# The values of a gated linear attention as one unit of seven half products

## The chip, the core and the metric

The kernel runs on one core of a Trainium2 chip, in one launch. The metric is the device time in microseconds (us). Times of the kernel before are the median of three runs; durations and waits are read from one further execution that the hardware profiler recorded.

## The reference: what is computed

One layer of an encoder over 1024 tokens of 1024 features: a normalisation, one projection into queries, keys, values and gates, a gated linear attention of four heads in both directions, a pooling branch, a merge, and a feed-forward layer. The part that matters here:

```
h = rmsnorm(x, norm_mix)                       # 1024 tokens x 1024 features
q, k, v, r, lr_f, lr_b, u, g_a, g_b = split(h @ w_in)
#   q, k: 4 heads x 128;  v: 4 heads x 256 = 1024 columns
log_a_f = log_sigmoid(lr_f @ w_decay_up_fwd + b_decay_fwd) / 16      # and _b
o_fwd = gla_chunked(q, k, v, log_a_f)          # scan over chunks of tokens
o_bwd = flip(gla_chunked(flip(q), flip(k), flip(v), flip(log_a_b)))
# in each chunk:  o = (q_e k_e^T, masked) v + q_e S ;  S <- decay * S + k_d^T v
o = rmsnorm of o_fwd + o_bwd, times gla_norm * silu(r);   y_a = o @ w_branch_gla
```

All inputs and the output are float32. The values `v = h @ w_v` are a product of 1024 x 1024 by 1024 x 1024: this is the product that the change rebuilds.

## The kernel before

**Exact products from pairs.** TensorE multiplies in a shortened float type (`F32R`). Each operand is therefore kept as a high part and a low part: `split_to` (lines 200 to 202) has ScalarE (ACT) cast the tile to the high part (line 201), and then VectorE (DVE) or GpSimd (POOL) subtracts it to give the low part (line 202; for weights it is POOL, for most activations DVE). A product of two tiles is then three matmuls onto one PSUM bank, high x high, high x low, low x high: `products` and `mm3` (lines 270 to 277; line 273 is the matmul). In names `wh` and `wl` are high and low parts of weights, `hh` and `hl` of the normalised features, `trh` and `trl` of sums of features, `vh` and `vl` of values. The low part is wanted by the second or third matmul of each three.

**Order of the work.** Every engine runs its instructions in the order of the program. SyncE (SP) issues the DMA transfers, also in order, each with its waits. TensorE's order is written out by hand: loops over heads and token tiles. After each three matmuls `mm3` calls `pump` (line 162 on), which counts the time by units of one such product of 512 columns (about 0.7 us) and lets side work be issued: `pending` (splits of weights, one each 2 units), `aside` (a list of sums with casts and stores beside them), `side` (generators that yield the number of units to their next step, such as `attention`), and `put_off` (`soon`: one step after a delay). So a `yield 6.5` in `attention` places the next step 6.5 products later in every engine's queue.

**Storage.** Tiles of 128 x 1024 come from 39 rotating slots (`slots`). Weights stand in `wts` with 6 buffers for each of high and low and 4 raw ones. PSUM has 3 banks for products (`ps_mm`) and 5 for the rest (`ps_g`).

**The stages around the change.** The features `hT` are made first, feature-major (high and low), two token tiles at a time. Values of heads 0 and 1 (`pair_products`, lines 494 to 502) are computed as plain products, token tiles 0 to 3 while the features are still being made: 8 row blocks x 3 matmuls into one bank of 128 tokens x 512 columns, and `keep_values` (480 to 492) splits the bank into high (ACT, line 490) and low (DVE, line 492) for both heads. Then `first_qk` (1181 to 1197) makes the low-rank decay inputs (`low_rank`, 541 to 553) and queries and keys of head 0: four banks of 8 x 3 matmuls. Beside its second half runs `sums_behind`: `feature_sums` (683 to 706) lets VectorE add high and low parts of the features and form sums and differences of the blocks (128 x 1024 each, recorded with line 768, names `hs`), which are stored to HBM (`f_out`) for the gates' seven-product units much later. After that `attention(0)` begins as side work, token tiles 7, 6 and 5 to 4 of the values of heads 0 and 1 follow on TensorE, and `store_block` stores one block of the features. Then `sum_pieces` (beside the heads 1 and 2) makes sums of weights of the later stages on POOL (names `wsum` and `rraw`, line 768). `project_qk` (line 895 on) makes queries and keys of heads 1 to 3. The values of heads 2 and 3 come after head 2's queries and keys, from `ValueWeights` (line 793 on): eight tiles of 24 matmuls.

`attention(h)` (from line 926) runs through: decays (matmuls `z`, line 935, then absolute value, exponential and logarithm on ACT, with the `yield 6.5` behind), scans on DVE (`decay`, from 958), exponentials (`exponentials`, 981 to 990), the factors applied to keys and queries (`apply_decay`, 992 to 999: keys on DVE, `qe` and `fac` on POOL) spaced by `HOLD` units, the transposed keys (`kt`, split at line 202), the backward states (`advance`, from 1020, which needs the values of its chunk), the scores with `SCORES` units behind them, and the outputs. Before a chunk whose value tile is not there yet it yields until it is.

## Time and profile before

| | us |
|---|---|
| runs | 1361.23, 1361.35, 1362.74 |
| median | 1361.35 |
| profiled execution, its own time | 1361.08 |
| its span in the trace | 1359.4 |
| TensorE busy | 1348.2 |
| DVE busy | 850.1 |
| POOL busy | 813.4 |
| ACT busy | 652.0 |

The span goes from the first to the last instruction that the profiler recorded; the execution's own time is 1.7 us longer. The granted TensorE clock was 0.999 of full speed. An instruction is listed with its start, its length, its engine, the line, the operation, the output and input tiles, and in square brackets the time that the engine waited before it and for whom. A group row has the count, the busy time and the mean length in ns, then the idle time ahead of its instructions and what ended most of it. Matmul lengths in the list overlap: two that follow each other start closer than one is long.

### The profile page before, as it was taken

To read this page: it belongs to the slowest core of one execution; us is meant where nothing else is said; L and a number is where in the kernel's file an instruction comes from. 1 tells how busy PE (TensorE), PEld (TensorE's weight loads), DVE (VectorE), ACT (ScalarE), POOL (GpSimd) and SP (SyncE) were. 2 spreads that over 40 slices of the span, in tenths; PEclk is the share of its full clock that TensorE was granted. 3 is DMA by queue.
4 is the path that set the end of the run, shared out by engine and by line. 5 is a ranking of instruction groups with operands and counts; after the bars stand their busy time and mean duration, and the time that the engine had idled before them with its cause. 6 is when DMAs were issued, how large, how long until landed. Compare 5 with 4: busy or idle time off the path is not lost. (4 is left out here: it accounts for less than half of the span.)

```text
span 1359.4 us, 18038 instructions
## 1 busy us (share of the span) xinstructions
PE 1348.2 (99%) x6226; PEld 1121.4 (82%) x6226; DVE 850.1 (63%) x1049; ACT 652.0 (48%) x1184; POOL 813.4 (60%) x626
## 2 busy tenths in 40 slices
PE   9999999999999999999999999999999999999998
PEld 7888888888888888888887888888888888888886
DVE  6975667766436868669774955565565655343375
ACT  7365666776435445453356533333333333444253
POOL 3333847586686548568853476666667666555463
PEclk9999999999999999999999999999999999999999
DMA  7243647446896669986327454555554447975552
GB/s 229 106 146 113 187 138 219 143 143 205 265 303 218 206 212 333 384 333 243 101 78 260 131 165 147 164 178 178 178 177 141 133 143 261 394 283 186 173 215 78
DMA packets 194621, 268.26 MB, mean 197 GB/s; under 512 B 13112, under 2 KB 121184, under 8 KB 194528
## 3 DMA queue, kind: packets, MB, share of 16 engines
q1 hardware_dynamic: 194384, 266.83, 58.6%
q8 instruction: 49, 0.80, 0.2%
q14 instruction: 44, 0.36, 0.1%
q10 hardware_dynamic: 144, 0.26, 0.1%
HBM read 178.70 MB, written 88.34 MB: 196 GB/s over the span
## 5 line engine op out<-in xcount | busy, mean ns | idle before, releaser
L202 POOL TENSOR_TENSOR wl<-fs,wh 128x512 fp32r<-128x512 f32 x120 | 165.9, 1386 | 155.8 <-ACT wh L201 99.7
L273 PE MATMUL ps<-gh,wh 128*128 128x512 f32 x616 | 240.5, 390 | 0.0
L273 PE MATMUL ps<-gl,wh 128*128 128x512 f32 x616 | 239.8, 389 | 0.3 <-DVE gl L1870 0.3
L273 PE MATMUL ps<-gh,wl 128*128 128x512 f32 x616 | 239.7, 389 | 0.0
L202 POOL TENSOR_TENSOR wl<-fraw,wh 128x512 fp32r<-128x512 f32 x90 | 129.5, 1439 | 57.4 <-ACT wh L201 52.2
L202 POOL TENSOR_TENSOR ol<-gor,oh 128x1024 fp32r<-128x1024 f32 (+1 forms) x42 | 101.6, 2423 | 85.7 <-ACT oh L201 59.7
L273 PEld LDWEIGHTS ps<-gl,wh 128*128 128x128 f32 x616 | 115.7, 188 | 24.4 <-DVE gl L1870 0.7
L273 PEld LDWEIGHTS ps<-gh,wl 128*128 128x128 f32 x616 | 115.6, 188 | 24.1
L273 PEld LDWEIGHTS ps<-gh,wh 128*128 128x128 f32 x616 | 115.7, 188 | 24.0 <-DVE sums L2036 0.2
L273 PE MATMUL ps<-hh,wh 128*128 128x512 f32 x296 | 119.8, 405 | 0.4 <-ACT ga L1654 0.4
L202 POOL TENSOR_TENSOR wl<-wraw,wh 128x512 fp32r<-128x512 f32 x56 | 93.3, 1693 | 44.8 <-ACT wh L201 44.7
L273 PE MATMUL ps<-oh,oh 128*128 128x512 f32 x308 | 119.8, 389 | 0.0
L273 PE MATMUL ps<-ol,oh 128*128 128x512 f32 x308 | 119.8, 389 | 0.0
L273 PE MATMUL ps<-oh,ol 128*128 128x512 f32 x308 | 119.8, 389 | 0.0
L273 PE MATMUL ps<-hh,wl 128*128 128x512 f32 x296 | 115.5, 390 | 0.0
L273 PE MATMUL ps<-hl,wh 128*128 128x512 f32 x296 | 115.5, 390 | 0.0
L202 DVE TENSOR_TENSOR ol<-wor,oh 128x1024 fp32r<-128x1024 f32 (+1 forms) x42 | 62.7, 1504 | 67.7 <-ACT oh L201 55.2
L273 PE MATMUL ps<-trh,wh 128*128 128x512 f32 x224 | 88.9, 397 | 0.0
L273 PE MATMUL ps<-trh,wl 128*128 128x512 f32 x224 | 87.2, 389 | 0.0
L273 PE MATMUL ps<-trl,wh 128*128 128x512 f32 x224 | 87.2, 389 | 0.0
L201 ACT CAST wh<-fs 128x512 fp32r<-128x512 f32 x120 | 73.7, 614 | 26.7 <-DVE fs L1239 25.8
L201 ACT CAST oh<-wor 128x1024 fp32r<-128x1024 f32 (+1 forms) x42 | 41.1, 978 | 63.6 <-PE ps L273 24.2
(286 smaller groups left out, 3153.3 us busy)
## 6 DMA issues: line engine op xcount, KB each, us to landing
fraw<-in_w_ffn_in_dram SPq DMA_DIRECT2D x44, 512.0 KB, 6.9
gor<-g_out SPq DMA_DIRECT2D x35, 512.0 KB, 4.6
g_out<-s SPq DMA_DIRECT2D x44, 256.0 KB, 2.4
fraw<-in_w_in_dram SPq DMA_DIRECT2D x20, 512.0 KB, 5.7
wor<-t_out SPq DMA_DIRECT2D x20, 512.0 KB, 4.5
g_out<-g SPq DMA_DIRECT2D x33, 256.0 KB, 2.9
x<-in_x_dram SPq DMA_DIRECT2D x16, 512.0 KB, 4.5
wor<-in_w_ffn_out_dram SPq DMA_DIRECT2D x15, 512.0 KB, 7.7
```

Of the source, the lines that this page charges most:

```text
L201: nc.scalar.copy(hi, src)
L202: eng.tensor_tensor(lo, src, as_f32(hi), op=ALU.subtract)
L273: nc.tensor.matmul(ps, a[i], b[j], start=first and n == 0, stop=last and n == 2, skip_group_check=onto)
```

## The change

The values of all heads become one unit of Strassen's scheme (Winograd's form): the token tiles are two halves, the features two halves, and the 1024 columns two halves (heads 0 and 1, heads 2 and 3). Seven half products, each 4 token tiles x 4 row blocks x 512 columns, with sums of feature blocks and sums of weight blocks as operands, replace eight.

- Products 1 and 2 together are the plain values of token tiles 0 to 3 for heads 0 and 1, made at the start as before. Product 1's sum is now also copied out of the bank half way (`keep_first`, ScalarE), since other products need it.
- `values((5, 3, 6))` follows head 0's queries and keys, `values((7, 4))` head 1's. 5, 6 and 7 start new banks, 3 and 4 go on in the banks of the product before. `v_evict` adds a finished bank to the kept rows on VectorE or ScalarE, with a few sums on POOL.
- The weight sums of products 5, 7, 6 and 3 are made by `value_sums` on POOL: 16 sums of 128 x 512 (line 865 in the changed kernel), beside the second half of head 0's queries and keys. Of products 5 and 3 they stay on the chip, of 6 and 7 they are stored and reloaded.
- The feature sums are the same that the gates use. VectorE's list of them is reordered so that number 5 comes first; they are stored, reloaded (`load_sums`), cast on ACT (`cast_sum`) and their low parts made on POOL (`low_sum`, `trl`, line 768 of the changed kernel).
- Values of heads 1 to 3 are stored to HBM (`v_raw`), reloaded by `load_values` in their head's attention, cast on ACT (`high_values`) and their low part made on POOL (`low_values`, line 1059 of the changed kernel).
- The sums of weight pieces (`rraw`, `wsum`) begin at product 7, the `rraw` pieces first, instead of behind token tile 4.
- The block of features stored by `store_block` is stored at product 3 and reloaded in heads 1 and 2.
- In `attention`, `HOLD` goes from 5 to 4, `SCORES` from 6 to 5.5, the wait behind the logarithms from 6.5 to 4 units.
- `ValueWeights` and its stage of 8 tiles x 24 matmuls after head 2 are gone.

In counts of instructions: TensorE has 48 matmuls fewer (6106 to 6058), POOL 50 two-input operations more (579 to 629), ACT 16 copies and 2 casts more, VectorE 8 two-input operations fewer (732 to 724), SP 53 transfers more (758 to 811).

How the queues change is shown at three places. The first is POOL from the low parts of head 0's key weights (`wl_674` and `wl_684` before, `wl_684` and `wl_694` after) on. Before:

```order
L202 TENSOR_TENSOR wl_674<-raw_629,wh_673 128x512
L202 TENSOR_TENSOR wl_684<-raw_631,wh_683 128x512
L202 TENSOR_TENSOR wl_771<-raw_753,wh_770 128x512
L202 TENSOR_TENSOR wl_781<-raw_755,wh_780 128x512
L998 TENSOR_TENSOR qe_948<-qe_948,q_588 128x512
L999 TENSOR_TENSOR fac_949<-fac_949 128x4
```

After; `vsum` and `vraw` are the weight sums, `wl_806` and `wl_816` the low parts of head 1's query weights, `trl_787` and `trl_788` the low parts of the feature sums of product 5, and `wl_842` the low part of its first weight block:

```order
L203 TENSOR_TENSOR wl_694<-raw_641,wh_693 128x512
L865 TENSOR_TENSOR vsum_703<-vsum_699,vsum_703 128x512 x2
L865 TENSOR_TENSOR vsum_705<-vsum_701,vsum_705 128x512 x2
L865 TENSOR_TENSOR vsum_699<-vraw_140,vsum_699 128x512 x2
L865 TENSOR_TENSOR vsum_701<-vraw_143,vsum_701 128x512 x2
L865 TENSOR_TENSOR vraw_140<-vsum_703,vraw_140 128x512
L203 TENSOR_TENSOR wl_806<-raw_783,wh_805 128x512
L203 TENSOR_TENSOR wl_816<-raw_785,wh_815 128x512
...
L768 TENSOR_TENSOR trl_787<-trl_787,trh_835 128x1024
L768 TENSOR_TENSOR trl_788<-trl_788,trh_838 128x1024
L203 TENSOR_TENSOR wl_842<-vsum_703,wh_841 128x512
L203 TENSOR_TENSOR wl_846<-vsum_703,wh_845 128x512
```

Twelve sums and two large low parts have come in between; the rows left out are three of the sums. On TensorE the same place, the end of head 0's keys (`ps_798` before, `ps_849` after) and what follows. Before, the plain values of token tile 7:

```order
L273 MATMUL ps_798<-hh_600,wl_684 128x512
L273 MATMUL ps_833<-wv_214,hh_494 128x512 x2
L273 MATMUL ps_833<-wv_214,hl_495 128x512
L935 MATMUL z_838<-lrT_538,up_158 128x512
L273 MATMUL ps_833<-wv_227,hh_494 128x512 x2
```

After, product 5, with its four banks side by side and `z` the decays of head 0:

```order
L274 MATMUL ps_849<-hh_597,wl_694 128x512
L274 MATMUL ps_892<-wh_841,trh_835 128x512
L274 MATMUL ps_892<-wl_842,trh_835 128x512
L274 MATMUL ps_892<-wh_841,trl_787 128x512
L1071 MATMUL z_904<-lrT_543,up_158 128x512
L274 MATMUL ps_891<-wh_841,trh_835 128x512
```

The weights `wv` that stood on the chip since the start are replaced by `wh_841` and `wl_842`, made on the spot, and the second matmul of product 5 reads `wl_842`. The third place is POOL in attention of head 1. Before, where `wsum` are the pieces of the later stages and `wl` the value weights of heads 2 and 3 or the next head's:

```order
L998 TENSOR_TENSOR qe_1642<-qe_1642,q_1042 128x512
L999 TENSOR_TENSOR fac_1643<-fac_1643 128x4
L768 TENSOR_TENSOR wsum_1379<-wsum_1379 128x256
L768 TENSOR_TENSOR wsum_1600<-wsum_1600 128x256
L998 TENSOR_TENSOR qe_1685<-qe_1685,q_1042 128x512
L999 TENSOR_TENSOR fac_1686<-fac_1686 128x4
L768 TENSOR_TENSOR wsum_1600<-wsum_1600 128x256 x3
```

After, during products 7 and 4, where `trl_1719` and `trl_1720` are the low parts of the feature sums of product 4, `vl_1747` and `vl_1749` the low values of head 1 read back:

```order
L1059 TENSOR_TENSOR vl_1747<-vl_1747,vh_1838 128x1024
L1136 TENSOR_TENSOR qe_1828<-qe_1828,q_1277 128x512
L1137 TENSOR_TENSOR fac_1829<-fac_1829 128x4
L203 TENSOR_TENSOR wl_1858<-vr_1769,wh_1857 128x512
L768 TENSOR_TENSOR trl_1719<-trl_1719,trh_1811 128x1024
L817 TENSOR_TENSOR rraw_1795<-rraw_1795 128x2x128 x4
L1136 TENSOR_TENSOR qe_1828<-qe_1828,q_1277 128x512
L1137 TENSOR_TENSOR fac_1875<-fac_1875 128x4
L768 TENSOR_TENSOR trl_1720<-trl_1720,trh_1861 128x1024
L203 TENSOR_TENSOR wl_1909<-vr_1813,wh_1908 128x512
L817 TENSOR_TENSOR rraw_1849<-rraw_1849 128x2x128 x3
L1059 TENSOR_TENSOR vl_1749<-vl_1749,vh_1936 128x1024
```

Product weights, large low parts and pieces now share the stretch of head 1's query factors.

The core of the diff:

```diff
-    def pair_products(ts, before=None):
-        banks = [bank(ps_mm) for _ in ts]
+    def keep_first(t, ps):
+        nc.scalar.copy(v_first[t // 2][:, t % 2, :], ps[:, :])
...
+    def value_product(ps, t, k):
+        half = KT // 2
+        mm3(ps[:, :], tokens(hT(k, t // 4), t), pair_w[k], k == 0, k in (half - 1, KT - 1), k >= half)
+
+    def first_values():
+        banks = [bank(ps_mm) for _ in range(2)]
         for k in range(KT):
-            if before:
-                before(k)
-            for ps, t in zip(banks, ts):
-                mm3(ps[:, :], tokens(hT(k, t // 4), t), pair_w[k], k == 0, k == KT - 1)
-        for ps, t in zip(banks, ts):
-            keep_values((0, 1), t, ps)
+            first_steps(k)
+            for t, ps in enumerate(banks):
+                if k == KT // 2:
+                    keep_first(t, ps)
+                value_product(ps, t, k)
...
-    pair_products((0, 1), first_steps)
+    first_values()
...
+        b12, b11, b22, b21 = (0, 1), (0, 0), (1, 1), (1, 0)
+        stores = []
+        for jobs in (
+            ((b12,), (b11,), (5, b11, b12, b11)),
+            ((b22,), (7, b12, b22, b12), (6, b22, b22, b11)),
+            ((b21,), (4, b21, b21, b22)),
+        ):
+            for c in range(2):
+                for p, *of in jobs:
+                    if not of:
+                        restored(c, *p)
+                    else:
+                        diff(c, *of)
+                        stores.append([3, partial(store, p, c, of[0])])
+                    yield 1.6 if jobs[0] == (b12,) else 2.5
+                    for entry in stores:
+                        entry[0] -= 1
+                    while stores and stores[0][0] <= 0:
+                        stores.pop(0)[1]()
+        for _, step in stores:
+            yield 2
+            step()
...
-    HOLD, SCORES = 5.0, 6
+    HOLD, SCORES = 4.0, 5.5
+
+    V_RUN = 5, 3, 6, 7, 4
+    v_sequence = [(p, k) for p in V_RUN for k in range(4)]
...
+    def value_sums():
+        x21, x22 = ([value_rows(c, j) for c in range(2)] for j in range(2))
+        x11, x12 = vraw[:2], vraw[2:]
+        yield 4
+        for op, dst, x, y, p in (
+            (padd, x22, x21, x22, 5), (psub, x21, x11, x21, 7), (psub, x11, x22, x11, 6), (psub, x12, x12, x11, 3)
+        ):
+            for c in range(2):
+                for k in range(2):
+                    op(*(t[c][:, k, :] for t in (dst, x, y)))
+                    yield 2
+                if p in v_here:
+                    v_here[p].append(dst[c])
+                else:
+                    soon(4, partial(nc.sync.dma_start, v_out[p][:, 2 * c : 2 * c + 2, :], dst[c][:, :, :]))
...
+    def v_split(n):
+        if n < len(v_sequence):
+            p, k = v_sequence[n]
+            hi, lo = (wts.tile([P, HALF], F32R, tag=s, name=name(s))[:, :] for s in ("wh", "wl"))
+            src = v_here[p][k // 2][:, k % 2, :] if p in v_here else v_raws.pop((p, k))
+            split_to(hi, lo, src, nc.gpsimd)
+            v_parts[p, k] = hi, lo
...
+    def split_values(m, src):
+        hi, lo = (t[:, m, :] for t in values_of(0, 1))
+        nc.scalar.copy(hi, src)
+        nc.vector.tensor_tensor(lo, src, as_f32(hi), op=ALU.subtract)
+        v_tiles[0].add(4 + m)
...
+    def v_evict(p, m, ps):
+        at = {5: (1, 1), 3: (0, 1), 6: (0, 1), 7: (1, 1), 4: (1, 0)}[p]
+        if at not in v_rows:
+            v_rows[at] = [slot(s="vu") for _ in range(2)]
+        dst, u = row(at, m), row((1, 0), m) if (1, 0) in v_rows else None
+        if p in (5, 3):
+            nc.scalar.copy(dst, ps)
+            if p == 3:
+                soon(2, partial(padd, dst, dst, u))
+            return
+        add(dst, ps, dst)
+        if p == 6:
+            split_values(m, dst[:, :DV])
+            add(u, ps, u)
+            soon(3, partial(padd, row((1, 1), m), row((1, 1), m), u))
+            if m == 0:
+                soon(4, partial(store_values, 1, 1, v_rows.pop(at)), partial(put_rows, (1, 1)), partial(put_rows, (1, 0)))
+        elif m == 0:
+            rows = v_rows.pop(at)
...
+    def values(stages, steps, by_tile=()):
+        banks = []
+        for p in stages:
+            if p in (5, 6, 7):
+                banks = [bank(pool) for pool in [ps_mm] * 3 + [ps_g]]
+            at = [(m, k) for m in reversed(range(4)) for k in range(4)]
+            if p not in by_tile:
+                at.sort(key=lambda e: e[1])
+            for n, (m, k) in enumerate(at):
+                if n % 4 == 0:
+                    for step in steps.get((p, n // 4), ()):
+                        step()
+                mm3(
+                    banks[m][:, :], tokens(tuple(t[:, k % 2, :] for t in right[p][k // 2]), m), v_parts[p, k],
+                    k == 0 and p in (5, 6, 7), k == 3, p in (3, 4),
+                )
+                if k == 3:
+                    v_evict(p, m, banks[m][:, :])
...
+    def load_values(h):
+        for half in (1, 0):
+            lo = v_lows[h, half] = slot(F32R, (4, DV), "vl")[:, :, :]
+            nc.sync.dma_start(as_f32(lo), v_raw[h][half])
+
+    def high_values(h, half):
+        lo = v_lows.pop((h, half))
+        hi = slot(F32R, (4, DV), "vh")[:, :, :]
+        v_slots[h][half] = hi, lo
+        nc.scalar.copy(hi, as_f32(lo))
+
+    def low_values(h, half):
+        hi, lo = v_slots[h][half]
+        nc.gpsimd.tensor_tensor(lo, as_f32(lo), as_f32(hi), op=ALU.subtract)
+        v_tiles[h].update(range(4 * half, 4 * half + 4))
...
-        yield 6.5
+        yield 4
         flush()
+        if h:
+            load_values(h)
...
+        if h:
+            high_values(h, 1)
         yield 2
+        if h:
+            low_values(h, 1)
...
+                if half and not n:
+                    load_sums(5)
+                elif half:
+                    for c in range(2):
+                        cast_sum(5, c)
+                        low_sum(5, c, nc.gpsimd)
+                    while len(v_here[5]) < 2:
+                        next(other[0][0])
+                    v_splits(2)
...
+    v_steps = {
+        (5, 0): [splits],
+        (5, 1): [split],
+        (5, 2): [split],
+        (5, 3): [split],
+        (3, 0): [finish_other, store_block, split, partial(load_sums, 6), loads, loads],
+        (3, 1): [split, cast6[0]],
+        (3, 2): [split, cast6[1], low6[0]],
+        (3, 3): [split, low6[1]],
+        (6, 0): [split],
+        (6, 1): [fetch],
+        (6, 3): [prepare],
+        (7, 0): [begin_pieces, splits, loads, low7[1], partial(load_sums, 4), partial(load_rows_again, (1, 1))],
+        (7, 1): [split, v_loads],
+        (7, 2): [split, cast4[0], v_loads, partial(load_rows_again, (1, 0))],
+        (7, 3): [split, cast4[1], low4[0]],
+        (4, 0): [low4[1], split],
+        (4, 1): [fetch],
+        (4, 3): [prepare],
+    }
+    qk_steps = {
+        (1, 0, 0): [partial(load_sums, 7), loads],
+        (1, 0, 1): [loads, *cast7, low7[0], splits],
+    }
...
             begin(attention(h + 1))
         if h == 0:
-            for ts in ((7,), (6,), (5, 4)):
-                pair_products(ts)
-            store_block()
-            prepare_beside([sum_pieces(
-                [branch_piece_of(k, s) for k in range(4) for s in range(2)]
-                + [r_piece_of(u, c) for u in range(TRIO + 1) for c in range(2)]
-            )], 1.3, floor=-0.5)
-        if h == 2:
-            value_weights.pop().products()
+            v_loads(8)
+            values((5, 3, 6), v_steps, (6,))
+        elif h == 1:
+            values((7, 4), v_steps)
+            right.clear()
```

More of the change, by code (lines that the diff above doesn't have):

```diff
@@ L144 @@
     nc.gpsimd.memset(half_neg[:, :], -0.5)
-    side, aside = [], []
+    side, aside, other = [], [], []
     pending, credit = [], [0.0]
@@ L171, in pump @@
                 pending.pop(0)()
-        if aside:
-            aside[0][1] -= dt
-            if aside[0][1] <= 0 and not pending:
-                cost = next(aside[0][0], None)
-                if cost is None:
-                    aside.pop(0)
-                else:
-                    aside[0][1] = max(aside[0][1], aside[0][2]) + cost
+        for queue in (aside, other):
+            if queue:
+                queue[0][1] -= dt
+                if queue[0][1] <= 0 and not pending:
+                    cost = next(queue[0][0], None)
+                    if cost is None:
+                        queue.pop(0)
+                    else:
+                        queue[0][1] = max(queue[0][1], queue[0][2]) + cost
         if not side:
@@ new lines, with values_of, keep_values @@
+    v_next = []
+    def values_of(h, half):
+        if half not in v_slots[h]:
+            v_slots[h][half] = slot(F32R, (4, DV), "vh"), slot(F32R, (4, DV), "vl")
+        return v_slots[h][half]
+    def keep_first(t, ps):
+        nc.scalar.copy(v_first[t // 2][:, t % 2, :], ps[:, :])
+    def keep_values(t, ps):
+        hi, lo = (part[:, t % 4, :] for part in values_of(0, 0))
+        if not v_next:
+            v_next.append(slot(shape=(4, DV), s="vn"))
+        v_tiles[0].add(t)
+        nc.scalar.copy(hi, ps[:, :DV])
+        nc.scalar.copy(v_next[0][:, t, :], ps[:, DV:])
+        nc.vector.tensor_tensor(lo, ps[:, :DV], as_f32(hi), op=ALU.subtract)
+        if t == 3:
+            soon(3, partial(nc.sync.dma_start, v_raw[1][0], v_next.pop()[:, :, :]))
@@ L504, in first_steps, with next_values @@
+    next_banks = {}
+    def next_values(ks, before=None):
+        for t in (2, 3):
+            if t not in next_banks:
+                next_banks[t] = bank(ps_mm)
+            for k in ks:
+                if before and t == 2:
+                    before(k)
+                value_product(next_banks[t], t, k)
+            (keep_first if ks[0] == 0 else keep_values)(t, next_banks[t])
     def first_steps(k):
@@ L538 @@
     prepare()
-    pair_products((3,))
+    next_values(range(KT // 2, KT))
     masks()
@@ new lines @@
+    v_lows = {}
+    def load_values(h):
+        for half in (1, 0):
+            lo = v_lows[h, half] = slot(F32R, (4, DV), "vl")[:, :, :]
[9 more added lines that the diff above has]
+        v_tiles[h].update(range(4 * half, 4 * half + 4))
```

246 lines of the change are left out of this document (130 added, 116 removed).

## Prediction

> **What bounds the kernel now.** I read the page first, then who TensorE waited for, then the timelines of TensorE, GpSimd (POOL) and VectorE (DVE) over the stretch that is rebuilt, then the groups by engine. The page and the list of waits:
>
> ```profile
> span 1359.4 us, 18038 instructions
> PE 1348.2 (99%) x6226; PEld 1121.4 (82%) x6226; DVE 850.1 (63%) x1049; ACT 652.0 (48%) x1184; POOL 813.4 (60%) x626
> ...
> POOL 3333847586686548568853476666667666555463
> ```
>
> ```profile
> PE warm L461 <- POOL ident masks.py:199: 1.4, 1, 1.4
> PE tr L326 <- DVE xn L309: 0.9, 1, 0.9
> PE op L273 <- DVE kt L202: 0.7, 1, 0.7
> ```
>
> TensorE is busy for all but 11.2 us, and its longest wait in the run is 1.4 us. So the time is the sum of what TensorE issues: a matmul taken out is worth its place in the queue, and a wait put in is paid in full. No other engine is near its limit over the run. But POOL's slices run from 3 to 8 tenths: 3 in the first four (0 to 136 us), where the change adds to it.
>
> What one matmul is worth stands in TensorE's timeline, in the second half of head 0's query and key products, first and last of 48:
>
> ```profile
> 56.21 0.39 PE L273 MATMUL ps<-hh,wh 128*128 128x512 f32 x1
> ...
> 66.86 0.39 PE L273 MATMUL ps<-hh,wl 128*128 128x512 f32 x1
> 67.09 0.62 PE L273 MATMUL ps<-wv,hh 128*128 128x512 f32 x2
> ```
>
> A matmul is listed with 0.39 us, but they overlap: 47 starts from 56.21 to 66.86 are 0.2266 us apart. That, and not 0.39, is the price.
>
> **The change, part by part.** *The gain.* All values cost 8 token tiles x 8 row blocks x 2 column halves x 3 = 384 matmuls before; seven half products cost 7 x 4 x 4 x 3 = 336. The 48 that go are worth 48 x 0.2266 = **10.9 us**. TensorE has nothing else to gain.
>
> *The first two products.* The first product's partial sum is now copied out of a bank while the bank is still in use. The nearest row is ScalarE's copy of a bank:
>
> ```profile
> L1385 ACT COPY r<-ps 128x512 f32<-128x512 f32 x12 | 7.1, 595 | 8.1 <-PE ps L273 8.1
> ```
>
> The other bank's three matmuls (0.68 us) cover 0.60 us of copy except for the tail of the last matmul (0.39 - 0.23 = 0.16) and a signal: 0 to 1, I take **0.3 us**.
>
> *Product 5 (the first wait).* It follows the key product that ends at 67.09, and its second matmul needs `wl_842`, which POOL makes. The order shows what POOL does before it, from the low parts of head 0's key weights on: 5 splits and 12 sums of 128x512, and two low parts of 128x1024. Before, only the first two of these and two more splits stood there. What they cost, and when POOL can begin:
>
> ```profile
> L2070 POOL TENSOR_TENSOR wot<-wot 128x512 f32<-128x512 f32 x11 | 14.3, 1296 | 0.0
> ...
> L719 POOL TENSOR_TENSOR trl<-trl,trh 128x1024 fp32r<-128x1024 f32 x6 | 14.5, 2423 | 0.0
> ```
>
> ```profile
> 45.34 3.52 POOL L202 TENSOR_TENSOR wl<-raw,wh 128x512 fp32r<-128x512 f32 x2 [7.54 <-ACT wh L201]
> 58.92 3.69 POOL L202 TENSOR_TENSOR wl<-raw,wh 128x512 fp32r<-128x512 f32 x2 [10.07 <-ACT wh L201]
> ```
>
> ```profile
> 45.66 4.28 DVE L768 TENSOR_TENSOR hs<-hh,hl 128x1024 f32<-128x1024 f32 x2
> 49.97 1.23 DVE L768 TENSOR_TENSOR hs<-hs,hs 128x1024 f32<-128x1024 f32 x1
> ```
>
> POOL cannot begin before 45.34: it sat 7.54 us until ScalarE had cast those weights, and the instructions ahead of that cast are the same. Alone it would need 17 x 1.30 + 2 x 2.42 = 26.9 us, to 72.3: already 5.0 us after the second matmul's turn at 67.09 + 0.23 = 67.3. And it is not alone. The last fence shows VectorE's sixteen sums of features (128x1024), which stay: 1.23 us where POOL is idle, but two in 4.28 us beside two POOL operations, which took 3.52 instead of 2.6. From 45.34 to 49.94 two of each ran in 4.60 us: one at a time, in turn, 2.30 us a pair. With POOL's queue full, all sixteen sums now meet a POOL operation: 16 x 2.30 = 36.8 us to 82.1, then the two large low parts (4.8) and the split (1.3): 88.3. TensorE would wait 88.3 - 67.3 = **21.0 us** (5 if POOL were never held up).
>
> [...]
>
> *Products 5, 3 and 6 (the second wait).* From `wl_842` POOL has to reach `wl_1165`, the low part of the last block of weights of product 6, which that product's first token tile needs at its end. Between them the order has 11 splits, 6 sums and 3 query factors of 128x512, 2 low parts and 3 small factors:
>
> ```profile
> L998 POOL TENSOR_TENSOR qe<-qe,q 128x512 f32<-128x512 f32 x16 | 22.2, 1385 | 26.9 <-ACT qe L987 26.9
> ...
> L999 POOL TENSOR_TENSOR fac<-fac 128x4 f32<-128x4 f32 x16 | 6.9, 431 | 0.0
> ```
>
> 20 x 1.30 + 2 x 2.42 + 3 x 0.43 = 32.1 us. TensorE issues 105 matmuls, four for the decays and eight small transposes in that time: 109 x 0.2266 + 8 x 0.11 = 25.6. So it waits at least 6.5 us. Some of POOL's operations also wait for ScalarE, which loads its tables twice and copies four banks there; I take **8 us** (6.5 to 12).
>
> *Values of product 6 (a chain put in).* Attention of head 0 now takes each value tile as soon as it is made: one block's three matmuls (0.68 us) later. The chain is an add from the bank, a cast and a subtraction:
>
> ```profile
> L1659 DVE TENSOR_TENSOR ga<-ps,ga 128x512 f32<-128x512 f32 x33 | 22.7, 688 | 39.6 <-PE ps L273 39.5
> ...
> L490 ACT CAST vh<-ps 128x256 fp32r<-128x256 f32 x32 | 10.1, 389 | 4.2 <-PE ps L273 4.1
> ...
> L492 DVE TENSOR_TENSOR vl<-ps,vh 128x256 fp32r<-128x256 f32 x32 | 11.7, 417 | 7.7 <-ACT vh L490 7.7
> ```
>
> 0.69 + 0.39 + 0.42 + 0.16 = 1.66 us against 0.68 + 0.11: about 0.9 us a tile, 1 with signals, **4 us** for four (0 to 6). Behind those matmuls stand the next products.
>
> *Products 7 and 4 (the third wait).* POOL's first split for product 7's third block (`wl_1707`) cannot begin before ScalarE has copied the last key bank (0.60) and cast it (0.62). From there to `vl_1749`, the low values that attention of head 1 needs in product 4, the order gives POOL 6 splits, 3 query factors, 5 operations of 128x1024 (two of them the values read back from HBM), 3 small factors and 15 sums of 128x256, which stood elsewhere before:
>
> ```profile
> L768 POOL TENSOR_TENSOR rraw<-rraw 128x256 f32<-128x256 f32 x32 | 24.6, 776 | 1.5
> ```
>
> ```profile
> L201 ACT CAST wh<-raw 128x512 fp32r<-128x512 f32 x22 | 13.4, 622 | 6.2 <-DMA raw<-in_w_in_dram 6.2
> ...
> L912 ACT ACTIVATE k<-ps 128x512 f32<-128x512 f32 x6 | 3.6, 597 | 0.0
> ```
>
> 9 x 1.30 + 5 x 2.42 + 3 x 0.43 + 15 x 0.776 = 36.7 us, and 1.2 ahead of it. TensorE's work in between is 75 matmuls, 12 of half width and 8 transposes: 17.0 + 1.4 + 0.9 = 19.3. It waits 36.7 + 1.2 - 19.3 = 18.6; I take **18 us** (0 if the 15 sums and the low values were there early; 24 if their loads are late).
>
> *Nothing for the rest.* Head 2's old stage of eight splits goes, VectorE loses work, HBM traffic grows by some tens of transfers; none of it is waited for in the list of waits, and after the three waits TensorE is so late that the later stages have more slack than before. If that cover is gone it costs a few us.
>
> **How the numbers follow.** The sum is made against the profiled execution's own 1361.1 us (span 1359.4, and 1.7 around it), 0.3 under the median of the runs. 1361.1 - 10.9 + 0.3 + 21.0 + 8 + 4 + 18 = 1401.5; I say 1401. About 0.2% (2.7 us) is what a measurement can tell from no change.
>
> **The rivals.** (1) *POOL binds, but less*: VectorE's sums do not hold POOL up, and the first wait is 5.0 instead of 21.0: 1385. For it: only four pairs are seen in this stretch. Against it: each of them ran in turn. Likewise, if the third wait is not there: 1383. Together 0.22.
>
> (2) *Faster*: POOL keeps up, and TensorE is only relieved: 1361.1 - 10.9 + 0.3 = 1350.5. The place is POOL's queue from 45.34 on. It decides where POOL's operations between 45.34 and `wl_1165` (59.0 us by the rows) fit into TensorE's 67.3 - 45.3 + 25.6 = 47.6: they would have to be a fifth shorter than any row shows, and those of the third stretch by half. 0.05.
>
> (3) *The waits cost more than their length*, since TensorE is slow after a rest:
>
> ```profile
> 1.42 4.94 PE L461 MATMUL warm<-ident 128*128 128x128 f32 x24 [1.42 <-POOL ident masks.py:199]
> ...
> 12.16 1.03 PE L326 MATMUL tr<-ident,xn 128*128 128x128 f32 x8
> 12.95 0.70 PE L273 MATMUL ps<-wv,hh 128*128 128x512 f32 x2
> ```
>
> At the start, 24 transposes took 0.206 us each; later ones take (12.95 - 12.16) / 8 = 0.099. So a cold start costs up to 24 x 0.107 = 2.6 us, and four waits that are long enough would add 10: 1411. Against it: no wait in this trace is long enough to show it. 0.15. [...]
>
> (4) No difference, the waits happening to be as long as the gain: 0.02. That the change does not do what it says is excluded by the order: 48 matmuls fewer.
>
> The forecast itself (all three waits, 1390 to 1408) gets 0.56. The range takes in (1) and (3): 1378, where POOL alone binds at its shortest (waits of 5.0, 6.5 and 17, no chain), to 1418. Faster 0.05, same 0.02, slower 0.93.
>
> **What would show it right or wrong.** In the profile of the changed kernel, TensorE should wait for POOL's `wl`, `trl` and `vl` in some five places between 67 and 210 us, the longest of about 20 us at 67; POOL should be busy without a break from 45 us to its end; VectorE's `hs` sums there should last about 2.2 us each. If VectorE's sums last 1.2 us and POOL's 1.3 side by side, the first term is wrong. If TensorE's first long wait is for a DMA or ScalarE, POOL was not the last. If TensorE shows no wait over 2 us, the whole forecast is wrong, and the time is near 1350.

## The result and the profile after

The changed kernel takes 1443.07 us (median of four runs, 1440.85 to 1445.09) against 1361.45 for the kernel before (four runs, one more than in the table ahead): a ratio of 1.0597, with a 95% interval of 1.0579 to 1.0615. It is 82 us slower. The forecast was 40 us slower, with a range that ended at 1418. The sign was right, the size half.

The profiled execution took 1443.94 us. From its page, the span, the engines' busy time, and the rows of POOL and of the granted clock in 40 slices of 36 us:

```profile
span 1442.1 us, 18115 instructions
...
PE 1362.2 (94%) x6178; PEld 1124.4 (78%) x6178; DVE 864.5 (60%) x1041; ACT 671.3 (47%) x1202; POOL 901.1 (62%) x676
...
POOL 3787185686847855666876347666666668455454
PEclk9978989979999999999999999999999999999999
```

The page alone tells the two halves of the loss. TensorE has 48 matmuls fewer and should be busy 1348.2 - 10.9 = 1337.3 us; it is busy 1362.2, which is 24.9 more: what it issues took longer. It is idle 1442.1 - 1362.2 = 79.9 us, where it was idle 11.2: 68.7 more. 24.9 + 68.7 - 10.9 is the 82.7 by which the span grew. The clock's row shows where: its digits fall within the first nine slices, up to 325 us. A 9 stands for 90% or more, so a short fall can hide in one.

Who TensorE waited for (total, times, longest), and the four longest waits with their places:

```profile
PE ps L274 <- POOL wl L203: 17.9, 5, 12.2
PE ps L274 <- POOL trl L768: 17.2, 3, 14.5
PE kv L274 <- POOL vl L1059: 11.4, 4, 5.4
PE kv L274 <- ACT kt L202: 7.1, 1, 7.1
PE ps L274 <- ACT wh L202: 6.6, 1, 6.6
```

```profile
74.22 0.80 PE L274 MATMUL ps<-wh,trh 128*128 128x512 f32 x1 [6.59 <-ACT wh L202]
87.19 0.79 PE L274 MATMUL ps<-wl,trh 128*128 128x512 f32 x1 [12.17 <-POOL wl L203]
...
216.09 0.79 PE L274 MATMUL ps<-wh,trl 128*128 128x512 f32 x1 [14.55 <-POOL trl L768]
...
293.68 0.58 PE L274 MATMUL kv<-vh,kt 128*128 128x256 f32 x1 [7.11 <-ACT kt L202]
```

Before, the longest wait was 1.4 us; POOL's `trl` and `vl` were in no row, and its `wl` in one of 0.2 us. The first two lines of the second fence are the first wait, at product 5: 6.6 + 12.2 = 18.8 us, where 21.0 was forecast. POOL over that stretch, and one of VectorE's sums:

```profile
58.12 8.95 POOL L865 TENSOR_TENSOR vsum<-vraw,vsum 128x512 f32<-128x512 f32 x4
...
69.24 4.45 POOL L203 TENSOR_TENSOR wl<-raw,wh 128x512 fp32r<-128x512 f32 x2
73.65 6.69 POOL L865 TENSOR_TENSOR vraw<-vsum,vraw 128x512 f32<-128x512 f32 x3
80.30 5.61 POOL L768 TENSOR_TENSOR trl<-trl,trh 128x1024 fp32r<-128x1024 f32 x2
85.87 2.49 POOL L203 TENSOR_TENSOR wl<-vsum,wh 128x512 fp32r<-128x512 f32 x2
```

```profile
57.04 2.20 DVE L720 TENSOR_TENSOR hs<-hs,hs 128x1024 f32<-128x1024 f32 x1
```

Each operation of POOL on 128x512 takes 2.2 us there and each sum of VectorE 2.2, as the forecast had it from four pairs. The low part that product 5 needs, the first of the last row, was ready at 87.1; the forecast said 88.3.

The terms of the sum, one by one (the parts of a row are from the timeline of TensorE; the price of the 48 matmuls can't be measured apart and is the forecast's):

| term | forecast | measured |
|---|---|---|
| 48 matmuls | -10.9 | -10.9 taken |
| copy of product 1's sum | 0.3 | no wait |
| first wait (product 5) | 21.0 | 18.8 |
| second wait (product 6) | 8 | 6.3 in three waits (2.09, 1.80 and 2.45) |
| chain of value tiles | 4 | 2.3: 0.9 for `vl`, 1.4 in three for `vh` |
| third wait (products 7 and 4) | 18 | 19.6 in four (0.98, 0.84, 14.55 and 3.25) |
| others up to product 4's end | 0 | 2.4 + 1.2 + 0.7 = 4.3 |
| waits in heads 2 and 3 | 0 | 17.0 |
| more busy time for what is issued | 0 | 24.9 |

The forecast's five terms for waits came to 51 and measured 47. What is missing is in the last three rows: 46 us. Of the 24.9, some 20 us are the clock: it stood at 0.50 in eight stretches between 72 and 376 us, TensorE was busy for 39.7 us of them, and half of that is lost. The other 5 aren't placed one by one; a matmul that stands alone beside a wait is listed with up to 0.80 us, where one in a row costs 0.2266.

### The profile page after: what moved, and what is told of

The parts are those of the page before. It is cut to its first block, busy times and chain, and to the rows that moved or that the text cites. A ratio compares the mean times of both kernels' runs of the same rounds, so it can differ in the third digit from the quotient of the medians.

```text
span 1442.1 us, 18115 instructions
## 1 busy us (share of the span) xinstructions
PE 1362.2 (94%) x6178; PEld 1124.4 (78%) x6178; DVE 864.5 (60%) x1041; ACT 671.3 (47%) x1202; POOL 901.1 (62%) x676
## 5 line engine op out<-in xcount | busy, mean ns | idle before, releaser
L274 PE MATMUL ps<-hh,wh 128*128 128x512 f32 x296 | 123.1, 416 | 1.9 <-DVE vu L924 1.2
L274 PE MATMUL ps<-trh,wl 128*128 128x512 f32 x224 | 87.2, 389 | 0.0
L274 PE MATMUL ps<-trl,wh 128*128 128x512 f32 x224 | 87.2, 389 | 0.0
```

The lines of the kernel that those rows point to most:

```text
L274: nc.tensor.matmul(ps, a[i], b[j], start=first and n == 0, stop=last and n == 2, skip_group_check=onto)
```

## The experiments

Theory: POOL's queue and what hangs on it makes the waits, and a wait costs, beyond its length, the time that TensorE runs slow behind it. Rivals: late transfers make the waits; the closer steps of attention make those in heads 2 and 3; a wait costs only its length. All runs but the last three had the kernel before beside them at 1362.0 to 1362.4, the last three at 1362.5. The changed kernel's own runs spread over 4 us, so a difference of less than 3 us in a median isn't told from none; there the trace decides.

### What a wait costs beyond its length

**Stalls in the kernel before.**

```diff
+def stall(src, width):
+    d = slot(s="stall")
+    q, k = qk_heads[0]
+    nc.gpsimd.tensor_tensor(d[:, 0, :width], src, src, op=ALU.add)
+    for _ in range(3):
+        nc.gpsimd.tensor_tensor(d[:, 1, :], k[:, 1, :], k[:, 1, :], op=ALU.add)
+    ps = bank(ps_mm)
+    nc.tensor.transpose(ps[:, :P], d[:, 1, :P], ident[:, :])
 for ts in ((7,), (6,), (5, 4)):
+    stall(...)   # on the last tile that TensorE's work has given, key or value
     pair_products(ts)
```

> The kernel before, with three stalls put in: ahead of token tiles 7, 6 and 5 TensorE waits for a tile that POOL, idle there, makes by four sums (5.2 us, or 4.7 with a narrow first one, and about a microsecond of hand-over). No other work is added. Theory (a wait costs more than its length, since the granted clock falls in it): three waits of 5.5 to 6.5 us, and behind each of them matmuls 0.43 instead of 0.23 us apart, 2 to 3.5 us lost each: 1361 + 18 + 8 = 1387 us. Rival (a wait costs its length): the matmuls behind are 0.23 apart, 1379.

1385.85 us, ratio 1.0178 (1.0162 to 1.0193): 23.7 us more. The three waits are 16.6 us in all:

```profile
PE ps L1206 <- POOL stall L1204: 16.6, 3, 6.4
```

TensorE's busy time rose from 1348.2 to 1354.5 us, 6.3, though only three transposes were added; the clock stood at 0.50 for 3.4 to 6.8 us around the end of each wait. So a wait cost about 2 us on top of itself. The theory's 1387 was near, the rival's 1379 was not.

**Shorter stalls.**

```diff
-    for _ in range(3):
+    for _ in range(n):   # 1, 1 and 2
```

> The kernel before with three shorter stalls at the same places as in the run with stalls: one POOL sum less or two, so that TensorE waits about 3.8, 2.4 and 3.7 us. Theory (waits of some 2 us already bring the clock down, so that the many short waits of the changed kernel cost as much as the long ones): 2 us or more lost behind each of the three, 1361 + 10 + 6 = 1377 us. [...]

1378.70 us, ratio 1.0125 (1.0108 to 1.0142): 16.2 us more, of which 10.2 are the waits (4.2, 2.7 and 3.3). TensorE around the second of them, and the granted clock there by the microsecond:

```profile
83.72 0.33 PE L1206 MATMUL ps<-ident,stall 128*128 128x128 f32 x1 [2.74 <-POOL stall L1204]
83.81 0.83 PE L273 MATMUL ps<-wv,hh 128*128 128x512 f32 x2
84.43 0.63 PE L273 MATMUL ps<-wv,hl 128*128 128x512 f32 x1
84.86 1.05 PE L273 MATMUL ps<-wv,hh 128*128 128x512 f32 x2
```

```profile
83.00:84.00 1.00, 0.28 (x2) 1.00 0.00 0
84.00:85.00 1.00, 1.00 (x5) 0.63 0.00 0
85.00:86.00 1.00, 1.00 (x4) 0.50 0.00 0
86.00:87.00 1.00, 1.00 (x4) 0.50 0.00 0
87.00:88.00 1.00, 1.00 (x4) 0.67 0.00 0
```

The number behind the bracket is the clock, and the one before the bracket TensorE's busy time. The clock was still full when TensorE began again at 83.7, fell to 0.50 within the next microsecond and came back before 88: matmuls 0.43 instead of 0.23 us apart, 1.7 us lost behind 2.7 us of waiting. A wait of 2.7 us cost clock too.

The traces show more than the length of the wait at work. In the changed kernel the eight slow stretches begin at 72.5, 120.3, 188.5, 205.6, 229.5, 290.9, 304.6 and 372.9 us; each lasts 3.41 us or a whole multiple of it (six times that for the first), and the distances between them are such multiples too. So in this trace the clock changes at the marks of a grid of 3.41 us. The same wait of 2.37 us, for ScalarE's copy of head 1's key bank, cost clock in the changed kernel (the first two rows, two steps of its grid) and none in the run with 160 transposes below (the other two rows), where it lay across a mark:

```profile
185.12:188.53 3.41, 1.39 (x7) 1.00 0.79 227
188.53:191.94 3.41, 3.06 (x7) 0.50 0.90 275
```

```profile
183.50:186.92 3.42, 1.96 (x8) 1.00 0.60 159
186.92:190.33 3.41, 2.50 (x11) 1.00 0.99 337
```

TensorE was busy for 1.39 us of the step ahead of the fall, and for 1.96 and 2.50 us of the two steps that the other wait shares. In the changed kernel (its first 20 and last 30 us aside) it was busy for 0 to 1.39 us of the step ahead of each of the eight falls, and for 1.97 us or more of each step at full clock that none followed. So what such a wait of 2.37 us costs is in part luck of its place.

**The first wait filled with work.**

```diff
+            if p == 5:
+                for i in range(160):   # 182 in the second run
+                    nc.tensor.transpose(banks[3][:, i % 4 * P : (i % 4 + 1) * P], ident[:, :], ident[:, :])
```

> 160 transposes of the unit matrix (17.4 us at 0.109 each) are put ahead of product 5, into a bank that product 5 overwrites: TensorE works where it waited 18.8 us, and nothing else moves. Theory (a wait costs 3.6 us more than its length, since the granted clock halves in it and TensorE starts slow behind it): the 3.6 us of slow matmuls from 87 to 93 us go, and the time falls by 3 to 4 us to 1439.5. Rival (a wait costs its length alone): no change, 1443, or more by what the transposes overrun.

1441.08 us (1440.05 to 1443.31; ratio 1.0583, 1.0568 to 1.0599). The wait that was left was 1.9 us, and behind it the clock still fell to 0.50, for 3.4 us. About 1 us was won at product 5: a third of what was expected.

> The first filling of the first wait left 2 us idle, and the clock still fell; here 182 transposes fill it to its end. Theory (a wait costs what the clock loses in it): no matmul of product 5 is 0.43 apart, product 5 ends 3 us earlier than in the changed kernel, about 1440 us. Rival: no change, 1443.

1441.81 us (1440.18 to 1442.72; ratio 1.0583, 1.0567 to 1.0599). The median alone can't tell that from the changed kernel. The trace can; the same stretch in the changed kernel, then in this one:

```profile
87.00:89.00 2.00, 1.81 (x4) 0.50 1.01 401
89.00:91.00 2.00, 2.00 (x6) 0.50 1.03 412
```

```profile
87.00:89.00 2.00, 2.00 (x12) 1.00 0.97 389
89.00:91.00 2.00, 2.00 (x10) 1.00 1.01 403
```

The clock stays at 1.00, and between 87 and 93 us 26 matmuls begin instead of 14 (a row counts those that reach over its edge, and the last transposes, as well). The long wait in product 4 ended at 212.9 us instead of 216.1, 3.2 earlier, and the span is 2.4 shorter. For this wait the theory holds.

### The first wait

**Sums of value weights early.** `value_sums` starts behind the first two token tiles; its first sum comes 15 units later.

```diff
+    other.append([value_sums(), 0.5, -1e9])
     first_values()
...
-        other.append([value_sums(), 0.5, -1e9])
```

> The sixteen sums of value weights on POOL begin behind the first two token tiles, where POOL idles, instead of beside head 0's queries and keys; their loads move with them. Eleven of them now stand ahead of the split that POOL begins at 45.7 us. Theory (POOL's queue is what ends last at products 5 and 6, and each POOL operation beside a VectorE sum costs a pair of 2.3 us): from 45.7 ten small and two large operations are left, 10 x 2.3 + 4.8 = 28 us, to 73.5, so the first wait shrinks from 18.8 us to about 6 and the second from 7 to under 3, with some of the slow clock behind them: 1443 - 13 - 5 - 4 = about 1421 us, products 7 and 4 unchanged. Rival (the first wait is set by transfers that are late, since ScalarE waited 10.3 us for the raw weights of head 1): the first wait stays above 15 us and the time above 1435.

1440.48 us, ratio 1.0572 (1.0557 to 1.0588). The wait at product 5 fell to 0.8 + 6.6 = 7.4 us, near the 6 of the theory, but not by its way:

```profile
75.41 0.49 PE L274 MATMUL ps<-wh,trh 128*128 128x512 f32 x1 [0.82 <-ACT wh L202]
82.51 0.79 PE L274 MATMUL ps<-wl,trh 128*128 128x512 f32 x1 [6.60 <-POOL wl L203]
```

The low part was ready only 4.7 us earlier (82.5 instead of 87.2, where 73.5 was expected); POOL, with fewer sums ahead of it, now waited 4.3 us for head 1's weights to be cast. The other 7.0 us of the shorter wait are TensorE's own delay: it came to product 5 at 74.6 instead of 67.6. For 3.5 us of a new wait stand at 51 us, for the weights of head 0's keys, whose load now stands in SP's queue behind stores of the sums. The second wait didn't move: 2.1, 1.8 and 2.4 us, though six sums were gone from the count by which it had been forecast. So its 8 was near by chance: POOL idles between (2.9, 1.2, 2.6 and 1.2 us for ScalarE's casts, up to 101 us), and what makes that wait is the stretch from about 100 us on, when ScalarE has given POOL its operands.

**VectorE's sums later.**

```diff
                     yield 1.6 if jobs[0] == (b12,) else 2.5
+                    if c and p == 5:
+                        yield 60
...
-        (5, 1): [split],
+        (5, 1): [finish_aside, split],   # issues the ten sums that are left
```

> Ten of VectorE's sixteen sums of features (all but those that product 5 needs) are put behind the first quarter of product 5; nothing of POOL moves. Theory (VectorE's sums and POOL's operations take turns): only six pairs are left in the first stretch, so ten POOL operations fall from about 2.2 to 1.3 us, the split wl of product 5 comes 8 to 9 us earlier, the first wait is about 10 us instead of 18.8; the second wait may grow, since the ten sums meet POOL there, by up to 6: 1434 to 1441 us. Rival (POOL's operations are that slow for another reason, DMA traffic or their own operands): 2.2 us each as before and a first wait of 18 us, 1443 or more.

1450.19 us, ratio 1.0646 (1.0628 to 1.0664). POOL where VectorE had its last sum at 66:

```profile
68.25 2.48 POOL L203 TENSOR_TENSOR wl<-raw,wh 128x512 fp32r<-128x512 f32 x2
70.69 3.71 POOL L867 TENSOR_TENSOR vraw<-vsum,vraw 128x512 f32<-128x512 f32 x3
```

3.71 us instead of 6.69 for three sums, 2.48 instead of 4.45 for two splits: 1.24 us each, not 2.2. The mechanism of the first term is shown: the low part was ready 6.9 us earlier, and the first wait fell to 8.2 + 3.7 = 11.9. The time rose all the same, since the ten sums then stood ahead of head 0's decays in VectorE's queue and TensorE waited 8.2 and 3.5 us for `ke`.

**Both, and transfers in another order.** With the low parts on VectorE as in the run further down, sums early, their stores 36 units behind instead of 4, and `fetch()` of head 1's weights ahead of `low_rank(1)`:

```diff
-                    soon(4, partial(nc.sync.dma_start, v_out[p][:, 2 * c : 2 * c + 2, :], dst[c][:, :, :]))
+                    soon(36, partial(nc.sync.dma_start, v_out[p][:, 2 * c : 2 * c + 2, :], dst[c][:, :, :]))
...
                 finish_side()
+                fetch()
                 low_rank(1)
```

> The same, and with the sums of value weights begun behind the first two token tiles, their stores put off and head 1's weights fetched ahead of the stores of feature sums, so that neither POOL's queue nor the order of the transfers holds product 5 up. Theory: the first wait falls from 18.8 to 5 us or less without the 3.5 us that the weights of head 0 waited when only the sums were moved: 16 to 20 us less than the run with the low parts on VectorE alone, about 1402. Rival (the first wait needs neither): within 6 us of that run.

1422.91 us, ratio 1.0447 (1.0432 to 1.0463), against 1422.18 for that run without it: no gain. The wait at product 5 is 10.9 + 5.4 = 16.3 us, where 5 or less was expected. POOL and ScalarE ahead of it:

```profile
78.46 5.63 POOL L805 TENSOR_TENSOR trl<-trl,trh 128x1024 fp32r<-128x1024 f32 x2 [10.60 <-ACT trh L801]
```

```profile
77.34 1.04 ACT L801 CAST trh<-trl 128x1024 fp32r<-128x1024 f32 x1 [12.26 <-DMA v_out<-vsum]
```

POOL is idle for 10.6 us, and ScalarE for 12.3, in front of the cast of product 5's feature sums, which come back from HBM (the profile names another transfer of the same queue). VectorE had begun on them some 6 us later, behind casts that took 4.6 us instead of 0.6 beside POOL's sums. So what is last at product 5 changes from run to run (POOL's queue, the order of the transfers, VectorE's sums with their way through HBM), and taking one away shows the next. The forecast's 21 was right in size and in what came last, but the wait isn't worth 21 to whoever relieves POOL alone.

### The third wait

**The values' loads first.**

```diff
+        if h:
+            load_values(h)
         for run in runs:
             nc.scalar.activation(zs[run][:, :], zs[run][:, :], AF.Exp, scale=-1.0)
...
         flush()
-        if h:
-            load_values(h)
```

> The changed kernel with the values read back in heads 1 to 3 ordered earlier: their loads stand ahead of the exponentials instead of behind the eight stores of the head before. Theory (POOL's queue, without a break from 198 to 216 us, is what ends last in product 4): ScalarE's wait of 7.2 us at 197 goes, but the wait of 14.6 us in product 4 stays above 10 and the time within 4 us of 1443. Rival (the values come back too late, and ScalarE's wait for them holds the casts behind it): the wait falls to 7 us or less, and those for vl in heads 1 to 3 (3.3, 5.4, 2.0) go too: 1425 us.

1444.74 us, ratio 1.0605 (1.0589 to 1.0621); the wait in product 4 is 14.0 us. ScalarE cast the values read back at 195.3 us instead of 203.9, without a wait (it then waited 5.9 us ahead of the next weights), and the long wait ended at 215.3 us instead of 216.1. The rival is out.

**The sums of pieces earlier, and later.**

```diff
-        (6, 3): [prepare],
+        (6, 3): [prepare, begin_pieces],
...
-        (7, 0): [begin_pieces, splits, loads, ...
+        (7, 0): [splits, loads, ...
```

> The sums of weight pieces begin at the end of product 6, not at product 7, so that a good part of them runs beside head 1's queries and keys, where POOL idles. Theory (15 of these sums stand in POOL's queue between the weights and the low values of products 7 and 4, and their transfers crowd SP in head 2): the wait of 14.6 us in product 4 falls to under 5, the 7.1 and 5.4 us in head 2 shrink by half or more, with their share of the slow clock: about 1415 us. Rival (the third wait is set by the values and sums read back from HBM): it stays above 10 us, 1435 or more.

1445.12 us, ratio 1.0611 (1.0595 to 1.0627): missed. The wait in product 4 grew to 18.8 us. There are 64 of these sums, not 15, and at their pace they still stood in products 7 and 4; now one of them waited 6.9 us for its load and held POOL's queue.

> The changed kernel with the sums of weight pieces begun behind product 4 instead of at product 7, so that none stands in POOL's queue, nor their transfers in SP's, during products 7 and 4. Theory (these sums are a third of what POOL does between the weights and the low values there): the wait of 14.6 us in product 4 falls to 5 or less and the 3.3 us for vl go; the waits of head 2 (7.1 and 5.4) stay or grow by a few: 1425 to 1435 us. Rival (the third wait is that of the values read back): it stays above 10.

Here `begin_pieces()` stands behind `values((7, 4), v_steps)`. 1443.70 us, ratio 1.0596 (1.0581 to 1.0612). The wait in product 4 fell to 7.7 us and the 3.3 for `vl` went, near what the theory said; those of head 2 went from 7.1 and 5.4 to 3.9 and 4.7. But a new one came in head 3:

```profile
PE kv L274 <- ACT kt L202: 18.6, 2, 14.6
```

14.6 us for the transposed keys, and the sum is as before. The sums of pieces carry their wait with them to the head in which they stand.

**Low parts on VectorE.**

```diff
-        return both(cast_sum, p, (0, 1)), both(low_sum, p, (0, 1), nc.gpsimd)
+        return both(cast_sum, p, (0, 1)), both(low_sum, p, (0, 1))
...
-        nc.gpsimd.tensor_tensor(lo, as_f32(lo), as_f32(hi), op=ALU.subtract)   # low_values
+        nc.vector.tensor_tensor(lo, as_f32(lo), as_f32(hi), op=ALU.subtract)
```

> The changed kernel with the low parts of the feature sums of products 6, 7 and 4 and of the values read back made by VectorE instead of POOL (ten operations of 128x1024, 2.4 us each on POOL). Theory (POOL's queue ends last from product 4 on, and a large low part there waits for all that stands ahead of it): the low part of product 4 comes right behind ScalarE's cast at 207.5, so the wait of 14.6 us falls to about 6; the waits for vl (3.3 in head 1, 5.4 in head 2, 2.0 in head 3) fall to under 1 each; with some of the slow clock about 1420 us. Rival (POOL is not the last: casts and transfers are as late, or VectorE is held up in turn): the sum of these waits falls by less than 8 us, 1435 or more.

1422.18 us, ratio 1.0444 (1.0429 to 1.0460): 21 us less, as expected. TensorE's waits for POOL's `vl` are gone, and the one in product 4 is half as long (the first row, at 204 us; the second is in head 2):

```profile
PE ps L274 <- ACT kt L202: 7.5, 1, 7.5
PE kv L274 <- ACT kt L202: 5.4, 1, 5.4
```

Twelve operations of 2.4 us moved (six `trl`, six `vl`; the expectation counted ten), and that was worth 21 us, with a VectorE that is 60% busy over the run.

### Heads 2 and 3

**No arithmetic for the pieces.**

```diff
-                yield partial(op, to, a, b), None, dst(p)
+                yield partial(lambda *tiles: None, to, a, b), None, dst(p)
```

> The changed kernel with the arithmetic of the sums of weight pieces left out (the pieces are loaded and stored as before, as they came, so that what is computed from them is not the reference's): POOL loses 64 operations of 0.78 us between 188 and 400 us, SP keeps every transfer. Theory for product 4 (POOL's queue): the wait of 14.6 us falls to 8 or less, that of 3.3 for vl goes. Theory for head 2 (the weights of the next head come late since SP's queue is full, and ScalarE, waiting for them, holds the transposed keys up): the wait of 7.1 us stays above 5, the one of 5.4 for vl goes. About 1425 us. Rival for head 2 (the closer steps, or POOL): the 7.1 us go as well, 1415 or less.

1422.13 us, ratio 1.0438 (1.0422 to 1.0454): 21 us less. The wait in product 4 fell to 10.1 (8 or less was expected), 3.3 for `vl` went. In head 2 the 7.1 us fell to 1.3 and the 5.4 to 1.6: here the rival was right that POOL makes them, though its time (1415 or less) was too low, and the theory that the transfers do it whatever POOL does was wrong. How, ScalarE's timeline of the changed kernel shows, some 14 us behind its copy of the key bank at 276.8:

```profile
290.64 0.62 ACT L202 CAST wh<-raw 128x512 fp32r<-128x512 f32 x1 [6.96 <-DMA raw<-in_w_in_dram]
...
293.06 0.57 ACT L202 CAST kt<-kp 128x512 fp32r<-128x512 f32 x1
```

And SP's waits for POOL between 235 and 290 us:

```profile
SPq L798 <- POOL rraw L817: 16.8, 5, 11.7
```

SP waits 16.8 us for POOL's sums of `rraw` in order to store them, the last of it at 265 us, and the weights of head 3 stand behind those stores; without the sums SP has no such wait there. ScalarE waits 7.0 us for these weights, and the keys of head 2, which TensorE wants, stand behind that in its queue. Without the sums the weights are cast 8.0 us behind the copy of the key bank, with them 13.8. A sum that nobody waits for stopped TensorE over three queues.

**The closer steps in the kernel before.** All three spacings, and the wait behind the logarithms alone:

```diff
-    HOLD, SCORES = 5.0, 6
+    HOLD, SCORES = 4.0, 5.5
...
-        yield 6.5
+        yield 4
```

> The kernel before with the attention's steps as close as in the changed kernel (4, 5.5 and 4 units instead of 5, 6 and 6.5), and nothing else of the change. Theory (POOL and the transfers put in are what is late, the spacing costs nothing by itself): within 3 us of 1361. Rival (the closer steps are what leaves the attention's chains of casts, scans and low parts too little time, so that TensorE waits in every head): 10 us or more on top, with waits for kt, ke and vl in heads 1 to 3.

1382.79 us, ratio 1.0146 (1.0128 to 1.0165): 20.7 us more, with nothing else of the change. The theory that the spacing is free fell.

```profile
PE kp L1015 <- DVE ke L997: 6.5, 4, 5.5
PE kv L273 <- ACT vh L490: 5.3, 2, 3.6
```

TensorE comes to the transposes and to the states before their operands are there, 5.5 us in head 2 and 3.6 in head 0. In the span of 1382.8 us its idle time grew by 14.0 us and its busy time by 9.4 (to 1357.6), of which some 7.4 are the clock: it stood at 0.50 in three stretches, behind waits of 3.6, 5.5 and 1.7 us.

> The kernel before with only the wait behind the logarithms cut from 6.5 to 4 units. Theory (all three spacings shift the attention's chains ahead of their operands, in proportion to the units taken out: 2.5 of about 6 in a head): 6 to 11 of the 21 us, 1367 to 1372. Rival (only the spacing between decays costs, since VectorE needs that time for the scans): within 3 us of 1362.

1369.96 us, ratio 1.0055 (1.0038 to 1.0072): 7.6 us more, within what was expected. By difference, the other 13 come from the other two spacings, which were not run without it.

**One spacing restored in the changed kernel.**

```diff
-        yield 4
+        yield 6.5
         flush()
```

> The changed kernel with the 6.5 units behind the logarithms restored (4 in the change); the other two spacings stay. Theory (the closer steps cost here what they cost in the kernel before, where all three made 21 us): 4 to 10 us less, 1433 to 1439, mostly in heads 2 and 3. Rival (in the changed kernel POOL and the transfers are later than the steps anyway): within 3 us of 1443.

1454.35 us, ratio 1.0678 (1.0662 to 1.0694): 11 us more; both theory and rival missed. The wait in product 4 fell to 10.1, but those for `vl` grew from 3.3 to 5.9 in head 1 and from 2.0 to 8.6 in head 3, and in head 2 a wait of 7.1 us for `ke` took the place of that for `kt`. In the changed kernel the steps and POOL's queue meet differently when the steps move, and the 21 us of the kernel before can't be carried over. No run restores all three. How much of its 17.0 us in heads 2 and 3 belongs to the spacing stays open.

## Why the forecast was half right

The step that failed is "Nothing for the rest", and with it the clock, which was kept out of the sum: 46 us where the forecast put none. The five terms that it did price came to 47 for 51.

- *The gain.* Right as a price: 48 matmuls at 0.2266 us. No run shows it apart.
- *Product 5.* Right in size and mechanism: POOL's operations and VectorE's sums at 2.2 us each beside each other (1.24 on POOL where VectorE's sums came later). It isn't what relieving POOL alone is worth, since other chains end close behind.
- *Products 5, 3 and 6.* 6.3 for 8 (and just under its bounds, 6.5 to 12), but by luck, from an account that counted POOL as busy through a stretch in which it waits: six sums taken away left it as it was.
- *The value chain.* 2.3 for 4, inside its bounds.
- *Products 7 and 4.* 19.6 for 18, and POOL's queue is the cause: loads made earlier did nothing, while without the sums of pieces the 14.6 us in it fell to 10.1, and with the low parts on VectorE to 7.5.
- *"Nothing for the rest"* failed. It argued that a late TensorE gives later stages more slack. It doesn't: in-order queues on POOL, SP and ScalarE carry POOL's delay into heads 2 and 3, where TensorE waits 17.0 us; 9.3 of the 13.2 in head 2 went with POOL's sums of pieces. It also passed over three numbers of the diff, `HOLD`, `SCORES` and the wait behind the logarithms, which alone cost the kernel before 20.7 us; the forecast gives them no term.
- *Rival (3), the clock*, was the other half. It was given 0.15 because "no wait in this trace is long enough to show it", and 10 us from the start of the program; it cost some 20 of the 24.9. It was no rival but a surcharge on the waits, behind short ones as well (one of 2.37 us). The trace has eight stretches at half clock that lost 1.5 to 4.8 us each, where four had been counted. Taken as a term of the sum, 1401 would have been 1411 by the forecast's own price; the rest needed the waits that were not seen.

So no wait that was priced was badly sized. The waits that were not looked for, and the surcharge, are as much as all that was. (The lower end of the range adds up to 1379, not 1378, which changes nothing.)

No run comes near the kernel before. The best two, with the low parts on VectorE and without the pieces' sums, are at 1422. The change can win 10.9 us at most.

## What to carry to other kernels

When TensorE is 99% busy, put a surcharge for the clock on the new waits, and count them, not only their sum: here a slow stretch cost 1.5 us or more, and one stood behind waits as short as 1.9 us (the first filling) and 1.7 us (the closer steps in the kernel before). Price every number that a diff changes, spacing constants too; one that only moves a step in the queues changes who is late for whom. And follow a loaded engine's stores: where another queue issues them in order, its delay comes out at loads that have nothing to do with it (here SP waited 16.8 us for POOL's sums, and ScalarE 7.0 for the next weights).

## What was not expected of the hardware

In the run with the shorter stalls the clock fell behind a stall of 2.7 us, and only after TensorE had begun again (0.63 in the microsecond from 84 on, with work since 83.7). In the changed kernel it came and went on a grid of 3.41 us, and each of its eight falls had a step ahead of it in which TensorE was busy for 1.39 us or less. And VectorE's casts of one operand took longer beside POOL as well: four casts of 128x128 took 0.62 us in the changed kernel and 4.55 where POOL's sums ran beside them, in the run with the sums early and the low parts on VectorE:

```profile
39.87 0.62 DVE L131 CAST keep<-keepf 128x128 uint8<-128x128 f32 x4
```

```profile
42.50 4.55 DVE L131 CAST keep<-keepf 128x128 uint8<-128x128 f32 x4
```

At the first wait POOL's operations on 128x512 and VectorE's sums beside them take 2.2 us each, where one alone takes 1.24 (POOL, in the run with VectorE's sums later) or 1.23 (VectorE, in the kernel before): less than the 2.47 of the two in a row.
